# First loads of a decoder block issued from two queues, and the passes of its first two k-tiles in another order

## The chip, the core and the metric

The kernel runs on one core of one Trainium2 chip. The metric is the device time of one execution, in microseconds; lower is better. Five engines work side by side, each through its own list of instructions in order: TensorE (PE in the profile, with its weight loads as PEld), VectorE (DVE), ScalarE (ACT), GpSimd (POOL) and SyncE (SP). They wait for each other by semaphores. Data come from device memory by DMA, through 16 DMA engines; a DMA is issued as an instruction on one engine's list, its queue.

## The reference

A decoder block with 512 tokens and a model width of 1024: two token mixers side by side, retention and forgetting attention, merged by gates, and then a SwiGLU feed-forward. What the change touches is the first line of it, the normalised input times the combined input projection:

```
h = rmsnorm(x, g_mix[l])
z = h @ w_in[l]
q_r, k_r, v_r, gt_r, q_f, k_f, v_f, f_f, a_r, a_f = split_cols(z)
```

The first group of columns that the kernel computes is q_r and k_r together, 512 columns for all 512 tokens.

## The kernel before

Matrix products run in a split form. Each float32 operand is taken apart into a high part, rounded to the format `float32r`, and a low part, the remainder; `three` (line 164) issues three matmuls, or passes, for one product: high x high, high x low and low x high. For the input that means `xh` and `xl`, for the weights `wh` and `wl` (`h` and `l` in the code).

The head of the kernel is lines 174 to 212. The input comes transposed, in NK = 8 k-tiles of 128 rows (`xT[:, k, :]`, 256 KB each). For each k-tile the loop at line 182 issues a load of x into `xf`, a load of 512 columns of weights into `raw` (for the last four k-tiles the buffer is called `spare`), and for the first k-tile a small load `ce`, 16 KB of constants that holds the scale `g_mix`. Then it makes four parts: ScalarE makes `xh` (line 189), VectorE makes `wh` (a cast, line 190), `xl` (line 191) and `wl` (line 194). All these loads are issued by SyncE, x and weights in turn.

Before them ScalarE does a copy of one element, `cold` (line 106), ahead of which a load of the activation table stands; TensorE runs eight warm-up matmuls on zeros (line 125).

The loop at line 196 then runs the products: for each of eight k-tiles and four token tiles t the three passes, 96 matmuls of 512 columns, into four accumulators (two banks called `sc`, two called `tp`). The program is laid out by a scheduler that sets the order of each engine's instructions by when it thinks that their inputs are there; only where `pinned[0]` is set does `in_order` (line 65) keep the matmuls in the order in which they are written. In the head it is not set.

After the head come the loads of the next group's weights (`ahead`, line 202), the input in row form for the sums of squares (`xs`, lines 203 to 207), and tables. The next group (`tok_group`, line 227) accumulates into banks called `acc`; its weights are split by ScalarE (line 151) and VectorE (line 152). Everything after that is the same in both kernels.

The buffers are reused by rotation: three pairs `wh` and `wl`, two `raw`, so that a cast for the next group waits until TensorE has read an older one. DMAs take eight semaphores in turn, so an issue can wait until an earlier load with the same semaphore has landed.

Of the kernel before, what the change touches and what calls it, by code (L numbers as in the profile page):

```python
# [17 lines left out]
P = 128  # L18
D = 1024
S = 512  # L20
NT = S // P
NK = D // P
# [31 lines left out]
def block_kernel(ctx: ExitStack, tc, x, xT, c_early, c_tab, c_late, w_qf, w_tok, w_a, w_y, w_o, w_gu, w_dn, out):  # L54
    nc = tc.nc
# [3 lines left out]
    pinned = [False, None]  # L59

    def after(ins, prev):

        tc.add_manual_dep(ins.ins, prev.ins.name, mybir.DependencyInfo(mybir.DependencyClass.NoSync, mybir.DependencyReason.DATA), reason="order")

    def in_order(ins):
        if pinned[0]:
            if pinned[1] is not None:
                after(ins, pinned[1])
            pinned[1] = ins

    def mm(o, **kw):
        in_order(nc.tensor.matmul(o, **kw))  # L72
# [4 lines left out]
    def f32(ap):  # L77
        return ap.bitcast(F32)
# [12 lines left out]
    def bank(tag):  # L91
        return ps.tile([P, 512], F32, name=tag, tag=tag, bufs={"acc": 4, "sc": 2, "tp": 2}[tag])

    ce = cst.tile([P, C_EARLY], F32, name="ce")
# [8 lines left out]
    nc.vector.memset(warm, 0.0)  # L103
    cold = sm.tile([P, 2], F32, name="cold", tag="cold", bufs=1)
    nc.gpsimd.memset(cold, 0.0)
    nc.scalar.copy(out=cold[:, 0:1], in_=cold[:, 1:2])
    ctab = cst.tile([P, C_TAB], F32, name="ctab")
    ident, tri, mask = (ctab[:, o:o + P] for o in (T_ID, T_TRI, T_MASK))

# [31 lines left out]
    def load_w(src, width=1024):  # L141
        pool, bufs = next_pool(raw_pools, 0)
        raw = pool.tile([P, WU if pool is wp else 1024], F32, name="raw", tag="raw", bufs=bufs)
        nc.sync.dma_start(out=raw[:, :width], in_=src)
        return raw
# [9 lines left out]
    def split_w(src, width=1024):  # L155
        return split_raw(load_w(src, width), width)

    def gmix(k):
        return ce[:, C_GMIX + k:C_GMIX + k + 1]
# [4 lines left out]
    def three(o, sh, sl, mh, ml, first, last):  # L164
        mm(o, lhsT=sh, rhs=mh, start=first, stop=False)
        mm(o, lhsT=sh, rhs=ml, start=False, stop=False)
        mm(o, lhsT=sl, rhs=mh, start=False, stop=last)
# [6 lines left out]
    xh = hp.tile([P, NK, S], F32R, name="xh")  # L174
    xl = hp.tile([P, NK, S], F32R, name="xl")
# [6 lines left out]
    for k in range(NK):  # L182
        u, cs = k // 2, slice(k % 2 * 512, k % 2 * 512 + 512)
        raw, xk, (h, l) = raws[u][:, cs], xf[k // 4][:, k % 4, :], first_units[u]
        nc.sync.dma_start(out=xk, in_=xT[:, k, :])
        if k == 0:
            nc.sync.dma_start(out=ce, in_=c_early)
        nc.sync.dma_start(out=raw, in_=w_tok[2, u, :, cs])
        act(out=xh[:, k, :], in_=xk, func=AF.Copy, scale=gmix(k))
        first = nc.vector.tensor_copy(out=h[:, cs], in_=raw)  # L190
        low = stt(out=xl[:, k, :], in0=xk, scalar=gmix(k), in1=f32(xh)[:, k, :], op0=ALU.mult, op1=ALU.subtract)
        if k == 0:
            after(low, first)
        tt(out=l[:, cs], in0=raw, in1=f32(h)[:, cs], op=ALU.subtract)
    accs = [bank(("sc", "tp")[t // 2]) for t in range(NT)]
    for k in range(NK):
        h, l = first_units[k // 2]
        cs = slice(k % 2 * 512, k % 2 * 512 + 512)
        for t in range(NT):
            tq = slice(t * P, (t + 1) * P)  # L200
            three(accs[t], xh[:, k, tq], xl[:, k, tq], h[:, cs], l[:, cs], k == 0, k == NK - 1)
    ahead = [load_w(w_tok[3, u]) for u in range(2)]
    for t2 in range(2):
        nc.sync.dma_start(out=xs[t2], in_=x[t2 * 256:(t2 + 1) * 256].rearrange("(t p) d -> p t d", p=P))
# [367 lines left out]
    cs = ftok.tile([P, NT, FH], F32, name="cs")  # L572
# [131 lines left out]
    accs = [bank(("tp", "sc", "acc", "acc")[b // 2]) for b in range(8)]  # L704
# [8 lines left out]
    for k in range(NF):  # L713
        h, l = split_w(w_dn[k])
# [109 lines left out]
```

## Time and profile before

| | us |
|---|---|
| median of 3 runs | 738.85 |
| lowest and highest run | 738.72, 739.54 |
| the profiled execution | 739.33 |
| its span, first to last instruction | 737.2 |

The profiled execution is one run with the hardware profiler; 2.1 us of its time lie outside the span. Times in a row are microseconds from the start of the span. The timeline gives start, duration, engine, line, operation and names (written to <- read from), and in brackets the idle time before it and what ended that. The profile pipelines matmuls: one takes longer than the distance to the next one's start, and the distance is what the engine can sustain. The chain of waits is followed back from the last instruction, at each step to what released it.

### The profile page before, as it was taken

The numbers are of one execution on the slowest core, as the hardware profiler recorded it, in microseconds if no ns is written. First come the engines' busy times: TensorE is split into PE (matmuls) and PEld (weight loads), VectorE is DVE, ScalarE is ACT, GpSimd is POOL, SyncE is SP. The second block draws the span as 40 slices with busy tenths as digits, with TensorE's granted clock in tenths as the row PEclk, the third lists the DMA queues.
The fourth block names the chain that finished last, engine by engine and source line by source line (L and its number), as shares of the span: only waits on it lengthen the run. The fifth ranks groups of instructions, "written<-read, shape, count | busy, mean of one in ns | idle before, by whom it ended". The sixth has DMA issues, their size and how long they took to land.

```text
span 737.2 us, 8828 instructions
## 1 busy us (share of the span) xinstructions
PE 729.2 (99%) x3430; PEld 596.5 (81%) x3430; DVE 367.6 (50%) x630; ACT 260.1 (35%) x389; POOL 108.8 (15%) x112
## 2 busy tenths in 40 slices
PE   8999999999999999999999999999999999999998
PEld 5888998778777788888888888888888887888886
DVE  6434567656878653454676343333333336323213
ACT  4532433347766732333433222222222233232210
POOL 0253502222211000000311110111110111000000
PEclk9999999999999999999999999999999999999999
DMA  8542222233321133336244223233232332332203
GB/s 315 202 123 78 88 76 62 68 121 105 104 73 55 36 107 93 108 86 222 92 143 135 94 86 114 86 100 101 87 110 90 94 107 85 97 104 85 86 0 115
DMA packets 23353, 76.20 MB, mean 103 GB/s; under 512 B 2696, under 2 KB 3080, under 8 KB 23312
## 3 DMA queue, kind: packets, MB, share of 16 engines
q1 hardware_dynamic: 23312, 75.64, 32.4%
q8 instruction: 27, 0.44, 0.2%
q14 instruction: 14, 0.11, 0.0%
HBM read 73.52 MB, written 2.11 MB: 103 GB/s over the span
## 4 chain that ended last, share of the span: by engine, by line
PE 92%; DVE 4%; ACT 2%; issue 1%; DMA 1%; SPq 0%; DVEq 0%; ACTq 0%
PE acc L72 76%; PE sc L72 9%; PE tp L72 6%; PE tp L75 2%; DVE wl L152 1%; ACT pr L482 1%; DMA xf<-in_xT_dram 1%; DVE pr L480 0%; ACT wh L151 0%; ACT pT L499 0%; DVE pr L484 0%; DVE tq L459 0%; ACT tq L458 0%; DVE og L382 0%; DVE up L688 0%
## 5 line engine op out<-in xcount | busy, mean ns | idle before, releaser
L151 ACT CAST wh<-raw 128x1024 fp32r<-128x1024 f32 (+1 forms) x118 | 123.8, 1052 | 381.4 <-PE acc L72 315.2
L152 DVE TENSOR_TENSOR wl<-raw,wh 128x1024 fp32r<-128x1024 f32 (+1 forms) x118 | 154.0, 1306 | 195.1 <-ACT wh L151 193.7
L72 PE MATMUL acc<-xgh,wh 128*128 128x512 f32 x352 | 137.4, 390 | 0.0
L72 PE MATMUL acc<-xgh,wl 128*128 128x512 f32 x352 | 136.9, 389 | 0.0
L72 PE MATMUL acc<-xgl,wh 128*128 128x512 f32 x352 | 136.9, 389 | 0.0
L72 PEld LDWEIGHTS acc<-xgh,wh 128*128 128x128 f32 x352 | 66.1, 188 | 13.9 <-issue 0.2
L72 PEld LDWEIGHTS acc<-xgh,wl 128*128 128x128 f32 x352 | 66.1, 188 | 13.8
L72 PEld LDWEIGHTS acc<-xgl,wh 128*128 128x128 f32 x352 | 66.1, 188 | 13.8 <-issue 0.2
L72 PE MATMUL acc<-wh,xh 128*128 128x512 f32 (+2 forms) x192 | 70.0, 364 | 0.0
L72 PE MATMUL acc<-wh,xl 128*128 128x512 f32 (+2 forms) x192 | 68.2, 355 | 0.0
L72 PE MATMUL acc<-wl,xh 128*128 128x512 f32 (+2 forms) x192 | 68.0, 354 | 0.0
L689 POOL TENSOR_TENSOR pf<-up,gt 128x512 f32<-128x512 f32 x22 | 38.2, 1756 | 199.3 <-DVE up L688 199.3
L72 PE MATMUL acc<-xh,wh 128*128 128x512 f32 x128 | 51.7, 404 | 0.0
L72 PE MATMUL acc<-xh,wl 128*128 128x512 f32 x128 | 50.0, 391 | 0.0
L72 PE MATMUL acc<-xl,wh 128*128 128x512 f32 x128 | 49.9, 390 | 0.0
L72 PEld LDWEIGHTS acc<-wh,xh 128*128 128x128 f32 x192 | 36.2, 188 | 5.5 <-issue 0.3
L72 PEld LDWEIGHTS acc<-wh,xl 128*128 128x128 f32 x192 | 36.2, 189 | 5.2
L72 PEld LDWEIGHTS acc<-wl,xh 128*128 128x128 f32 x192 | 36.2, 189 | 4.6
L72 PE MATMUL acc<-ph,wl 128*128 128x512 f32 x88 | 34.2, 389 | 0.0
L72 PE MATMUL acc<-pl,wh 128*128 128x512 f32 x88 | 34.2, 389 | 0.0
L72 PE MATMUL acc<-ph,wh 128*128 128x512 f32 x88 | 33.9, 389 | 0.0
L666 POOL TENSOR_TENSOR sqs<-sqs,sq 128x512 f32<-128x512 f32 x7 | 11.6, 1650 | 124.5 <-ACT sq L665 124.2
(215 smaller groups left out, 1121.8 us busy)
## 6 DMA issues: line engine op xcount, KB each, us to landing
raw<-in_w_gu_dram SPq DMA_DIRECT2D x44, 512.0 KB, 3.6
raw<-in_w_dn_dram SPq DMA_DIRECT2D x22, 512.0 KB, 3.6
raw<-in_w_tok_dram SPq DMA_DIRECT2D x16, 512.0 KB, 3.7
raw<-in_w_a_dram SPq DMA_DIRECT2D x16, 512.0 KB, 3.6
raw<-in_w_y_dram SPq DMA_DIRECT2D x8, 512.0 KB, 3.5
raw<-in_w_o_dram SPq DMA_DIRECT2D x8, 512.0 KB, 3.8
xf<-in_xT_dram SPq DMA_DIRECT2D x8, 256.0 KB, 5.4
xs<-in_x_dram SPq DMA_DIRECT2D x2, 1024.0 KB, 8.4
```

Of the source, the lines that this page charges most:

```text
L72: in_order(nc.tensor.matmul(o, **kw))
L75: in_order(nc.tensor.transpose(out=o, in_=src, identity=ident))
L151: nc.scalar.copy(out=h[:, :width], in_=raw[:, :width])
L152: tt(out=l[:, :width], in0=raw[:, :width], in1=f32(h)[:, :width], op=ALU.subtract)
L482: fox["last"] = act(out=pr[:, :n], in_=pr[:, :n], func=AF.Exp, scale=-1.0, bias=nm, accum_out=rs)
L666: gp.tensor_tensor(out=sqs, in0=sqs, in1=sq2, op=ALU.add)
L689: gp.tensor_tensor(out=pf[:, 2 * f2 + m2, :], in0=up, in1=gts[m2], op=ALU.mult)
```

## The change

The small load `ce` and the weights of the first four k-tiles are issued by ScalarE; x and the later weights stay on SyncE. The one-element copy on ScalarE stands behind its first two issues. The products of the first two k-tiles are written pass by pass over the four token tiles, in the order high x high, low x high, high x low (of x and weights), and the matmuls of the head are pinned to the written order.

```diff
--- before.py
+++ after.py
@@ -103,7 +103,6 @@
     nc.vector.memset(warm, 0.0)
     cold = sm.tile([P, 2], F32, name="cold", tag="cold", bufs=1)
     nc.gpsimd.memset(cold, 0.0)
-    nc.scalar.copy(out=cold[:, 0:1], in_=cold[:, 1:2])
     ctab = cst.tile([P, C_TAB], F32, name="ctab")
     ident, tri, mask = (ctab[:, o:o + P] for o in (T_ID, T_TRI, T_MASK))
 
@@ -184,8 +183,10 @@
         raw, xk, (h, l) = raws[u][:, cs], xf[k // 4][:, k % 4, :], first_units[u]
         nc.sync.dma_start(out=xk, in_=xT[:, k, :])
         if k == 0:
-            nc.sync.dma_start(out=ce, in_=c_early)
-        nc.sync.dma_start(out=raw, in_=w_tok[2, u, :, cs])
+            nc.scalar.dma_start(out=ce, in_=c_early)
+        (nc.scalar if k < 4 else nc.sync).dma_start(out=raw, in_=w_tok[2, u, :, cs])
+        if k == 0:
+            nc.scalar.copy(out=cold[:, 0:1], in_=cold[:, 1:2])
         act(out=xh[:, k, :], in_=xk, func=AF.Copy, scale=gmix(k))
         first = nc.vector.tensor_copy(out=h[:, cs], in_=raw)
         low = stt(out=xl[:, k, :], in0=xk, scalar=gmix(k), in1=f32(xh)[:, k, :], op0=ALU.mult, op1=ALU.subtract)
@@ -193,12 +194,19 @@
             after(low, first)
         tt(out=l[:, cs], in0=raw, in1=f32(h)[:, cs], op=ALU.subtract)
     accs = [bank(("sc", "tp")[t // 2]) for t in range(NT)]
+    pinned[0] = True
     for k in range(NK):
         h, l = first_units[k // 2]
         cs = slice(k % 2 * 512, k % 2 * 512 + 512)
-        for t in range(NT):
-            tq = slice(t * P, (t + 1) * P)
-            three(accs[t], xh[:, k, tq], xl[:, k, tq], h[:, cs], l[:, cs], k == 0, k == NK - 1)
+        tqs = [slice(t * P, (t + 1) * P) for t in range(NT)]
+        if k < 2:
+            for n, (a, b) in enumerate(((xh, h), (xl, h), (xh, l))):
+                for t in range(NT):
+                    mm(accs[t], lhsT=a[:, k, tqs[t]], rhs=b[:, cs], start=k + n == 0, stop=False)
+        else:
+            for t in range(NT):
+                three(accs[t], xh[:, k, tqs[t]], xl[:, k, tqs[t]], h[:, cs], l[:, cs], False, k == NK - 1)
+    pinned[0] = False
     ahead = [load_w(w_tok[3, u]) for u in range(2)]
     for t2 in range(2):
         nc.sync.dma_start(out=xs[t2], in_=x[t2 * 256:(t2 + 1) * 256].rearrange("(t p) d -> p t d", p=P))
```

ScalarE from its first instruction on (`junk` is the sum of squares, the CAST the split of the next group's weights). Before:

```order
L106 ACT_TABLE_LOAD
L106 COPY cold<-cold 128x1
L189 ACTIVATE xh<-xf,ce 128x512 x8
L151 CAST wh<-raw 128x1024 x2
L207 ACTIVATE junk,ss_85<-xs 128x1024 x4
```

The changed kernel:

```order
L186 DMA ce<-in_c_early_dram 128x32
L187 DMA raw<-in_w_tok_dram 128x512
L189 ACT_TABLE_LOAD
L189 COPY cold<-cold 128x1
L190 ACTIVATE xh<-xf,ce 128x512
L187 DMA raw<-in_w_tok_dram 128x512
L190 ACTIVATE xh<-xf,ce 128x512
L187 DMA raw<-in_w_tok_dram 128x512
L190 ACTIVATE xh<-xf,ce 128x512
L187 DMA raw<-in_w_tok_dram 128x512
L190 ACTIVATE xh<-xf,ce 128x512 x5
L150 CAST wh<-raw 128x1024
```

The weights of k-tiles 1 to 3 are each issued behind one `xh`; the table load stands behind two issues. Behind the last of these rows two sums of squares now come before the second CAST, and two after it.

VectorE from its first cast on: each k-tile has a CAST (`wh`), an `xl` and a `wl`. Before:

```order
L190 CAST wh<-raw 128x512
L191 SCALAR_TENSOR_TENSOR xl<-xf,ce,xh 128x512
L194 TENSOR_TENSOR wl<-raw,wh 128x512
L191 SCALAR_TENSOR_TENSOR xl<-xf,ce,xh 128x512
L190 CAST wh<-raw 128x512
L194 TENSOR_TENSOR wl<-raw,wh 128x512
L190 CAST wh<-raw 128x512
L191 SCALAR_TENSOR_TENSOR xl<-xf,ce,xh 128x512
L194 TENSOR_TENSOR wl<-raw,wh 128x512
```

The changed kernel:

```order
L191 CAST wh<-raw 128x512
L195 TENSOR_TENSOR wl<-raw,wh 128x512
L192 SCALAR_TENSOR_TENSOR xl<-xf,ce,xh 128x512 x2
L191 CAST wh<-raw 128x512
L192 SCALAR_TENSOR_TENSOR xl<-xf,ce,xh 128x512
L195 TENSOR_TENSOR wl<-raw,wh 128x512
L191 CAST wh<-raw 128x512
L192 SCALAR_TENSOR_TENSOR xl<-xf,ce,xh 128x512
L195 TENSOR_TENSOR wl<-raw,wh 128x512
```

For k-tile 0 `wl` now stands ahead of `xl`; for k-tile 1 `xl` stands ahead of the cast, and the `xl` of k-tile 2 ahead of the `wl` of k-tile 1. On SyncE five loads of x now come first, then weights and x in turn. On TensorE, after four high x high passes of k-tile 0, the other passes come in fours, for k-tile 1 too; from k-tile 2 on its order is what it was.

## Rows read from the trace of the kernel before

**Rows 1.** The page, parts 1 and 4: busy time by engine, the chain's shares by engine.

```profile
PE 729.2 (99%) x3430; PEld 596.5 (81%) x3430; DVE 367.6 (50%) x630; ACT 260.1 (35%) x389; POOL 108.8 (15%) x112
...
PE 92%; DVE 4%; ACT 2%; issue 1%; DMA 1%; SPq 0%; DVEq 0%; ACTq 0%
```

**Rows 2.** Windows: us, busy per engine (x instructions), granted clock, DMA share, GB/s.

```profile
9.76:28.68 18.92, 18.92 (x83) 15.69 (x84) 11.91 (x20) 9.78 (x14) 0.00 (x0) 1.00 0.98 385
```

**Rows 3.** The chain that ended last, in time: start us, us, what.

```profile
2.10 5.00 DMA xf<-in_xT_dram
```

**Rows 4.** Timeline of SyncE's queue: start us, us, engine, line, operation, names.

```profile
0.73 0.38 SPq L185 DMA_DIRECT2D xf<-in_xT_dram  x1
...
1.17 0.42 SPq L187 DMA_DIRECT2D ce<-in_c_early_dram  x1
...
1.64 0.42 SPq L188 DMA_DIRECT2D raw<-in_w_tok_dram  x1
...
2.58 0.43 SPq L188 DMA_DIRECT2D raw<-in_w_tok_dram  x1
```

**Rows 5.** DMA issues at 0.73, 1.17, 1.64, 2.10, 2.58: count, KB, us to landing.

```profile
xf<-in_xT_dram SPq DMA_DIRECT2D x1, 256.0 KB, 3.0
ce<-in_c_early_dram SPq DMA_DIRECT2D x1, 16.0 KB, 2.7
raw<-in_w_tok_dram SPq DMA_DIRECT2D x1, 256.0 KB, 3.2
xf<-in_xT_dram SPq DMA_DIRECT2D x1, 256.0 KB, 5.0
raw<-in_w_tok_dram SPq DMA_DIRECT2D x1, 256.0 KB, 5.2
```

**Rows 6.** Timeline of ScalarE.

```profile
0.73 1.28 ACT L106 ACT_TABLE_LOAD   x1 [0.73 <-PEq L813]
...
3.95 0.72 ACT L189 ACTIVATE xh<-xf,ce 128x512 fp32r<-128x512 f32 x1 [1.74 <-DMA ce<-in_c_early_dram]
...
7.13 0.72 ACT L189 ACTIVATE xh<-xf,ce 128x512 fp32r<-128x512 f32 x1 [2.46 <-DMA xf<-in_xT_dram]
...
23.44 1.05 ACT L151 CAST wh<-raw 128x1024 fp32r<-128x1024 f32 x1 [4.38 <-PE tp L72]
...
24.39 1.05 ACT L207 ACTIVATE junk<-xs 128x1024 bf16<-128x1024 f32 x1
```

**Rows 7.** Timeline of VectorE, first two k-tiles.

```profile
4.82 0.43 DVE L190 CAST wh<-raw 128x512 fp32r<-128x512 f32 x1 [3.69 <-DMA raw<-in_w_tok_dram]
...
5.16 0.74 DVE L191 SCALAR_TENSOR_TENSOR xl<-xf,ce,xh 128x512 fp32r<-128x512 f32 x1
...
5.83 0.68 DVE L194 TENSOR_TENSOR wl<-raw,wh 128x512 fp32r<-128x512 f32 x1
...
8.56 0.42 DVE L190 CAST wh<-raw 128x512 fp32r<-128x512 f32 x1
```

**Rows 8.** Timeline of TensorE, warm-up to the next group.

```profile
1.18 3.60 PE L72 MATMUL tp<-warm 128*128 128x512 bf16 x8 [1.18 <-DVE warm L103]
...
5.39 0.70 PE L72 MATMUL sc<-wh,xh 128*128 128x512 f32 x2 [0.61 <-DVE wh L190]
...
6.56 0.50 PE L72 MATMUL sc<-wl,xh 128*128 128x512 f32 x1
...
9.12 0.47 PE L72 MATMUL sc<-wh,xh 128*128 128x512 f32 x1 [0.46 <-ACT xh L189]
...
9.76 0.50 PE L72 MATMUL sc<-wl,xh 128*128 128x512 f32 x1 [0.16 <-DVE wl L194]
...
28.68 0.39 PE L72 MATMUL acc<-wh,xh 128*128 128x512 f32 x1
```

**Rows 9.** Windows of one microsecond, same columns as Rows 2.

```profile
5.00:6.00 1.00, 0.61 (x3) 0.55 (x4) 1.00 (x3) 0.00 (x0) 0.00 (x0) 1.00 0.54 160
...
9.00:10.00 1.00, 0.71 (x2) 0.43 (x3) 0.99 (x3) 0.38 (x2) 0.00 (x0) 1.00 1.06 397
```

## The prediction, made before the changed kernel ran

> **What bounds the kernel now.** I read first the page: TensorE is busy 99% of the span and 92% of the chain that ended last is its own [rows 1]. So the change can gain only where TensorE still waits, and it touches only the head, where the first group of projections is fed. The timeline of TensorE gives the size of that [rows 8]. Eight warm-up matmuls run from 1.18 to 4.78. The first real matmul starts at 5.39, the 96 matmuls of the group follow, and the next group starts at 28.68. From 9.76 on nothing stalls: 83 matmuls in 18.92 us, 0.228 us each [rows 2]. The 96 need 96 x 0.228 = 21.9 us; they got 28.68 - 5.39 = 23.3. So 1.4 us are stalls behind 5.39, and 0.6 us lie idle between 4.78 and 5.39: **2.0 us is all there is**, 0.27% of the time.
>
> Who ended those waits: the first matmul waited for the cast of the first weights [rows 8], which VectorE began at 4.82, as soon as they had landed [rows 7]. The second pass began at 6.56, when `wl` was made: 4 x 0.228 = 0.9 after 5.39 would have been 6.30. The eight matmuls from 6.56 end by 8.4, but k-tile 1 starts at 9.12, and its second matmul waits until 9.76 for the low part. The chain shows why: the second block of x, issued at 2.10, took 5.00 us [rows 3], `xh` of k-tile 1 starts only at 7.13 [rows 6], and VectorE's cast for k-tile 1 stands behind the `xl` that needs it, at 8.56 [rows 7]. With a stall-free run from k-tile 1 on, the end of the head stands as if k-tile 1 had started at 9.76 - 0.23 = **9.53**. The whole sum is the difference from that.
>
> **The change, part by part.** *Loads on two queues.* SyncE issues one load per 0.47 us (0.73, 1.17, 1.64) [rows 4]. Now `ce` and the first weights go out on ScalarE, at 0.73 and about 1.20 by the same spacing, and SyncE's first five rows are all blocks of x: the second goes from 2.10 to 1.17, 0.9 us earlier. Issue to landing was 3.0 to 3.2 us for the first loads, 5.0 and 5.2 for the next two [rows 5]. In one microsecond of that stretch the DMA engines moved only 160 GB/s, against 397 later [rows 9]; what caused that I can't see. First weights: not before 1.20 + 3.0 = 4.2, not after that plus the 256 KB of x beside them, which at 397 GB/s is 0.65: 4.85, what it was. I take 4.4, the 3.2 of the same load before. The first real matmul came 0.57 after the cast began [rows 7, 8], so it starts near 4.95, 0.4 earlier. If the first few then run at the warm-up's spacing of 3.60/8 = 0.45, that costs up to 0.9 us in the first pass; half of it is hidden by the wait that follows.
>
> *Table load behind the issues.* 1.28 us from 0.73 [rows 6], now from about 1.65, so ready by 3.1 with its copy. `xh` starts no earlier than its data, 0.73 + 3.0 = 3.73, so this is free with 0.6 to spare. `ce`, which ended the wait at 3.95, no longer decides.
>
> *Passes of k-tile 0.* TensorE now runs four high x high, four with `xl`, four with `wl`. But the order on VectorE is cast, `wl`, `xl`: the part needed second is made third. Either way both parts are wanted after four matmuls, so nothing is gained here: `wl` was started 1.01 after the cast and took 0.68, 1.69 in all [rows 7]; now `xl` is the last, 1.7 after 4.4, so the second pass starts at 6.1 and k-tile 0 ends at 6.1 + 8 x 0.228 = **7.9**. With the bounds of the landing: 7.7 to 8.4.
>
> *Weights of k-tile 1 behind `xh`.* This is the step that decides. The second weights were issued at 2.58 [rows 4]; now the issue stands on ScalarE behind the first `xh`. That one started at 3.95 and took 0.72 [rows 6], so the issue is at 3.95 if ScalarE's queue goes on while `xh` computes, 4.67 if not. No row shows a load issued on ScalarE. The Trainium skill (Perfetto Trace Analysis, section DVE / Act Engine Instruction) has the sequencer free for the next instruction once one is pushed into the wait queue; that would be 3.95; no row before shows it. Behind `xh`, too, stand the third and fourth weights, which k-tiles 2 and 3 need 2.7 and 5.5 us after k-tile 1: covered. From issue to landing the bounds are 3.2 (an idle queue, as the first weights) and 5.2 (as these very weights, with a backlog before them) [rows 5]. Its own queue is empty, though the engines still carry blocks of x, so I go a third of the way: 3.9, landing at 7.85. TensorE follows 0.57 later: **8.4**. Bounds: 3.95 + 3.2 + 0.57 = 7.7 and 4.67 + 5.2 + 0.57 = 10.4.
>
> *Passes of k-tile 1.* High x high and the `xl` pass cover 8 x 0.228 = 1.8 us. The low part of the weights is made after the cast and one `xl`, 1.69 behind the cast's start, and TensorE starts 0.57 behind it: cover 2.4 against 1.69. The stall between 9.12 and 9.76 is gone, and its return needs `xh` of k-tile 2 to be late by 0.7. K-tile 2 starts 12 x 0.228 = 2.7 after k-tile 1; VectorE makes three operations per tile, 1.7 us, and keeps ahead.
>
> *Behind the head.* On ScalarE the second cast for the next group, at 23.44 [rows 6], now stands behind two squares, 2 x 1.2 us. TensorE needs it 24 matmuls into that group, 28.68 + 5.5 = 34.2: covered by 7 us even if the head ends 2 us sooner. All else keeps its order; the gain passes to the end because TensorE has no further wait on anything of the head.
>
> **Sum.** K-tile 1 starts at max(7.9, 8.4) = 8.4 instead of 9.53: **1.1 us less**. The profiled execution took 739.33 (span 737.2 and 2.1 around it); with 1.1 less it would be 738.2. It lies 0.5 above the median of the runs shown, and against that median the forecast is 738.85 - 1.1 = 737.7. What a measurement of this kernel can tell from no change is about 0.2%, 1.5 us: the forecast is a gain below that.
>
> **Rivals.** *The early feed holds fully.* The second weights land by 7.3 and k-tile 0 is the bound: k-tile 1 starts at 7.7 to 7.9, a gain of 1.6 to 1.8 and at the very most the 2.0 of the whole, time 736.85 to 737.25. For it: the x blocks leave earlier and the new queue is empty. Against it: 3.2 us was seen only before the slow microsecond of [rows 9]. Chance 0.26.
>
> *Both queues issue one at a time.* The 0.47 us spacing is then shared: the first weights stand third or fourth, at 1.64 to 2.1, so the first matmul comes at 5.4 to 5.9 and k-tile 0 ends at 8.4 to 8.8; the second weights leave at about 4.4, land at 8.3 and k-tile 1 starts at 8.9. Gain 0.6; landing in 4.5 us instead of 3.9 leaves none: 738.25 to 738.85. For it: the 0.42 us of every issue row is spent somewhere [rows 4]. Against it: no row shows two queues at once. The Trainium skill names this mechanism (Perfetto Trace Analysis, section DMA Instruction — HWDGE (DVE, Sync)): the descriptor generator is shared and locked for exclusive use. By that rule two queues gain nothing in issue rate. A second sentence of the skill (DMA: Bandwidth & Descriptors, section Issuing engines are not separate DMA queues) says that issuing from several engines saves only the sequencer's time, usually small. Chance 0.22.
>
> *Slower: the second weights are late.* Their issue waits for `xh` to end (4.67), and the five blocks of x that SyncE sends off first, 1.25 MB or 3.3 us at 397 GB/s, go ahead of them. They land at 4.67 + 5.2 = 9.9, with another 0.65 to 2 us for the backlog at 10.5 to 11.9, and TensorE starts k-tile 1 at 11.1 to 12.5: 1.6 to 2.9 us slower, 740.4 to 741.8. It decides from a landing at 8.96: later than that is a loss. Against it: the engines would have to serve one queue before the other. Chance 0.05, and 0.03 for a milder form between 0 and 1.5 us slower.
>
> **How the numbers follow.** Forecast (gain 0.5 to 1.6) 0.44, full feed 0.26, one at a time 0.22, late weights 0.08. Faster by over 0.2% is most of the full feed and the best edge of the forecast: 0.23 + 0.05 = 0.28. Slower by over 0.2% is the late weights at their price: 0.05. Within: 0.67. The range reaches from the full feed's 736.85, rounded to 736.8, to a small loss of 0.25 us, 739.1; beyond it lie the late weights and the two ends, under 0.2.
>
> **What would show it.** Right: no wait on the first weights after 5.0, the `raw` issue on ScalarE at about 4.0, the cast of k-tile 1 near 7.9, the next group at 27.6 instead of 28.68, and no gap inside k-tile 1. One at a time: issue rows of near 0.9 us where both queues issue. Wrong: k-tile 1 past 9.53, or a new wait of TensorE behind 30 us.

## The result: slower, by a later and slower start

The changed kernel took 741.58 us (median of 8 runs, 740.22 to 742.2) beside 739.25 for the kernel before (8 runs, 738.72 to 740.72) on the same chip. The ratio is 1.0025, with a 95% interval of 1.0014 to 1.0036: slower by about 1.9 us, where 737.7 was forecast. (The ratio goes by the means of the runs; the medians are 2.3 us apart.) Every later run was timed beside the kernel before on its own chip, where that kernel's median lay between 739.3 and 739.9, so it is the ratios that can be set side by side. The profiled execution took 741.52 (span 739.6), against 739.33 (span 737.2) before.

All of it is lost in the head. The next group of projections starts at 31.32 instead of 28.68 [rows 8], 2.64 later; from there to the end the changed kernel needs 710.20 us (741.52 - 31.32), the kernel before 710.65, 0.45 less. The timeline of TensorE after (start, duration, engine, line, operation, names, idle time before and its releaser):

```profile
...
6.84 1.19 PE L72 MATMUL sc<-wh,xh 128*128 128x512 f32 x2 [2.06 <-DVE wh L191]
7.83 1.05 PE L72 MATMUL tp<-wh,xh 128*128 128x512 f32 x2
...
12.10 0.76 PE L72 MATMUL sc<-wh,xh 128*128 128x512 f32 x2
...
31.32 0.39 PE L72 MATMUL acc<-wh,xh 128*128 128x512 f32 x1
```

Three things differ from [rows 8]. The first real matmul comes at 6.84 instead of 5.39, after 2.06 us of idleness. The matmuls that follow stand as far apart as the warm-ups: k-tile 0 takes 12.10 - 6.84 = 5.26 us, 0.56 from the first matmul to the second and 0.427 for each of the next eleven, where 0.228 is the rate of [rows 2]; 512 columns in 0.427 us are 1.2 GHz, the lower of the two levels. And from 12.10 on nothing stalls, as the last of these stretches shows (busy time and count of TensorE first, then the other engines, granted clock, DMA share, GB/s):

```profile
4.78:6.84 2.06, 0.00 (x0) 0.03 (x1) 0.54 (x2) 0.77 (x2) 0.00 (x0) 1.00 1.01 383
6.84:12.10 5.26, 5.26 (x13) 4.10 (x14) 4.04 (x8) 2.74 (x4) 0.00 (x0) 1.00 1.04 386
12.10:31.32 19.22, 19.22 (x85) 15.91 (x84) 12.65 (x28) 7.95 (x12) 0.00 (x0) 1.00 0.83 313
```

So k-tile 1 starts at 12.10 and not at the effective 9.53: 2.57 of the 2.64. The clock column prints 1.00 in the middle stretch, as it does over the warm-ups; there the distance of the matmuls tells the level, not the column.

Who was waited for stands on ScalarE's and VectorE's timelines after, to be held against [rows 5 to 7]:

```profile
0.74 0.40 ACTq L186 DMA_DIRECT2D ce<-in_c_early_dram  x1
1.17 0.45 ACTq L187 DMA_DIRECT2D raw<-in_w_tok_dram  x1
1.65 1.28 ACT L189 ACT_TABLE_LOAD   x1 [1.65 <-PEq L821]
...
4.11 0.72 ACT L190 ACTIVATE xh<-xf,ce 128x512 fp32r<-128x512 f32 x1 [0.97 <-DMA ce<-in_c_early_dram]
4.11 0.35 ACTq L187 DMA_DIRECT2D raw<-in_w_tok_dram  x1
```

```profile
6.27 0.43 DVE L191 CAST wh<-raw 128x512 fp32r<-128x512 f32 x1 [5.14 <-DMA raw<-in_w_tok_dram]
...
9.60 0.43 DVE L191 CAST wh<-raw 128x512 fp32r<-128x512 f32 x1 [0.85 <-DMA raw<-in_w_tok_dram]
```

The first weights were issued half a microsecond earlier than before and landed 1.45 later. The DMA issues after, of the first 1.6 us and of 4 to 5 us (count, KB each, median us from issue to landing):

```profile
xf<-in_xT_dram SPq DMA_DIRECT2D x2, 256.0 KB, 3.8
raw<-in_w_tok_dram ACTq DMA_DIRECT2D x1, 256.0 KB, 5.1
ce<-in_c_early_dram ACTq DMA_DIRECT2D x1, 16.0 KB, 3.3
...
raw<-in_w_tok_dram ACTq DMA_DIRECT2D x1, 256.0 KB, 5.5
```

My theory behind the result: (a) the weights on the second queue share the DMA engines with five blocks of x that SyncE now sends off at once, four of which nobody needs yet; (b) the longer idleness after the warm-ups leaves TensorE at 1.2 GHz for the first pass. Rivals: ScalarE's queue is slow in itself; the new order of the passes costs; the second weights are late only because their issue stands behind `xh`.

### The profile page after: what moved, and what is told of

Read it like the earlier page. It is cut to its first block, busy times and chain, and to the rows that moved or that the text cites. A ratio compares the mean times of both kernels' runs of the same rounds, so it can differ in the third digit from the quotient of the medians.

```text
span 739.6 us, 8826 instructions
## 1 busy us (share of the span) xinstructions
PE 731.0 (99%) x3430; PEld 598.5 (81%) x3430; DVE 366.8 (50%) x630; ACT 259.9 (35%) x389; POOL 109.1 (15%) x112
## 4 chain that ended last, share of the span: by engine, by line
PE 96%; DVE 2%; DMA 1%; ACT 1%; issue 0%; ACTq 0%; DVEq 0%
PE acc L72 78%; PE sc L72 10%; PE tp L72 6%; PE tp L75 2%; DMA raw<-in_w_tok_dram 1%; ACT wh L150 0%; DVE wl L151 0%; DVE og L390 0%; DVE up L696 0%; DVE pl L726 0%; DVE n4a L120 0%; DVE n4a L119 0%; DVE n4y L121 0%; ACT pr L490 0%; DVE og L396 0%
```

## The experiments

### Which half of the change costs

`e1_loads_only` has the loads of the changed kernel and the loop of matmuls of the kernel before, not pinned. `e2_passes_only` has the loads of before and the new loop.

> The two queues of the changed kernel with the matmul order of the kernel before (no pinning, three passes per token tile). Theory: the first weights land late because ScalarE's queue shares the DMA engines with the blocks of x, TensorE idles about 2 us after its warm-up (4.8 to 6.8), and then runs its first matmuls at half rate, 0.427 us apart, as in the warm-up, until about 12.3. So this kernel is slow too: next group at 31.0 to 31.6, time 2 to 2.7 us over the kernel before. Rival: the new order of the passes makes the matmuls slow; then the matmuls here are 0.228 apart, the next group starts at 28.7 to 29.2, and the time is that of before within 0.5.

> The loads of the kernel before (all on SyncE) with the new pinned order of the passes. Theory: first real matmul near 5.4 as before, all matmuls 0.228 apart, the wait inside k-tile 1 (9.12 to 9.76) gone, next group at 28.0 to 28.4, time 0.3 to 0.7 below the kernel before, too little to be told from no change. Rival (the order of the passes is slow): matmuls of the first two k-tiles 0.427 apart, next group after 30.5, 2 us slower.

The loads alone: 740.39 us, ratio 1.0015 [1.0006, 1.0025], 1.1 us slower where I had expected 2 to 2.7. The first weights land 4.9 us behind their issue, the first matmul starts at 6.64 and the first eight matmuls run at the low clock, where the changed kernel had twelve; the next group starts at 30.23 and not past 31.0, as I had expected.

```profile
6.06 0.43 DVE L191 CAST wh<-raw 128x512 fp32r<-128x512 f32 x1 [4.94 <-DMA raw<-in_w_tok_dram]
6.64 1.19 PE L72 MATMUL sc<-wh,xh 128*128 128x512 f32 x2 [1.86 <-ACT xh L190]
```

The passes alone: 739.25 us, 0.9993 [0.9984, 1.0002], no difference that can be told. The passes are not the loss. But I had expected full rate from the first matmul and a next group by 28.4, and in the profiled execution the first eight matmuls were 0.43 apart, with the feed of the kernel before and only 0.72 us of idleness:

```profile
5.50 1.19 PE L72 MATMUL sc<-wh,xh 128*128 128x512 f32 x2 [0.72 <-DVE wh L190]
6.49 1.05 PE L72 MATMUL tp<-wh,xh 128*128 128x512 f32 x2
7.34 1.05 PE L72 MATMUL sc<-wh,xl 128*128 128x512 f32 x2
...
9.05 0.68 PE L72 MATMUL sc<-wl,xh 128*128 128x512 f32 x2
```

The next group came at 29.10. So the level of the clock behind the warm-ups is not settled by the idle time alone.

### How much is the clock

```diff
-WARM = 8
+WARM = 16   # in the changed kernel: e3_after_warm16
+WARM = 3    # in the kernel before: e4_before_warm3
```

> The changed kernel with 16 warm-up matmuls instead of 8, so that TensorE is busy until shortly before the first weights are there. Theory (the clock): the first real matmul still starts near 6.8, but runs at full rate; the next group starts at 28.7 to 29.0 instead of 31.32, and the time is 2.3 to 2.7 us under the changed kernel, that of before within 0.4. If the warm-ups run beyond 6.8 it is later by as much. Rival (something else than the idle time makes the first passes slow): still 0.427 apart until 12.3, no gain over the changed kernel.

> The kernel before with 3 warm-up matmuls instead of 8: only the idle time of TensorE ahead of the first real matmul grows, from 0.6 to about 2.9 us, loads and passes are untouched. Theory: the first real matmul starts at 5.4 and runs at 0.427 us spacing for several us; next group at 30.5 to 31.4, time 1.8 to 2.7 us over the kernel before. Rival (the loads or the passes are the cause, not the idle time): 28.7 and no change.

With 16 warm-ups the changed kernel takes 740.13 us, 1.0007 [0.9998, 1.0017]: from 1.9 us of loss some 0.5 is left, and that can no longer be told from none. TensorE runs at full rate from its first real matmul on, and what remains is the late data:

```profile
1.18 4.94 PE L72 MATMUL tp<-warm 128*128 128x512 bf16 x16 [1.18 <-DVE warm L103]
6.49 0.70 PE L72 MATMUL sc<-wh,xh 128*128 128x512 f32 x2 [0.37 <-ACT xh L190]
...
7.79 0.73 PE L72 MATMUL sc<-wh,xl 128*128 128x512 f32 x2
...
9.96 0.70 PE L72 MATMUL sc<-wh,xh 128*128 128x512 f32 x2
...
13.49 0.50 PE L72 MATMUL sc<-wl,xh 128*128 128x512 f32 x1 [0.30 <-DVE wl L195]
```

K-tile 1 starts at 9.96, still behind 9.53, and k-tile 2 waits for `wl` until 13.49; the next group starts at 29.72 and not by 29.0, as I had expected. Late data cost 29.72 - 28.68 = 1.04 here, so about 1.6 of the 2.64 went with the clock. Holding the clock alone does not make the change a gain.

In the other direction the kernel before with three warm-ups, 2.9 us idle and its own loads, runs twelve matmuls at 0.43 and starts the next group at 29.91, 1.23 later: 740.2 us, 1.0007 [0.9997, 1.0016].

```profile
5.55 1.19 PE L72 MATMUL sc<-wh,xh 128*128 128x512 f32 x2 [2.90 <-DVE wh L190]
...
29.91 0.39 PE L72 MATMUL acc<-wh,xh 128*128 128x512 f32 x1
```

The price of the low clock appears in the head without any of the change, though less of it than the 1.8 to 2.7 us that I had expected, and in the time it is too small to be told from none. Both runs change the amount of warm-up work together with the idle time, so they show what the clock costs and not which of the two sets it.

Then both kernels once more, unchanged:

> The kernel before, unchanged, profiled a second time. If the level of TensorE's clock behind the warm-up is settled by the program, the next group starts at 28.7 again and the first matmuls are 0.228 us apart, as in the first profile. If it differs from one execution to the next, the first eight to twelve matmuls may now be 0.427 apart and the next group starts up to 1.5 us later, near 30.

> The changed kernel, unchanged, profiled a second time. If the landing of the first weights, 5.1 us behind their issue, is settled by the two queues, it is 5.0 to 5.2 again and the cast of the first weights starts near 6.2. If it was an accident of one execution, it is nearer 3.5. The next group starts at 31.3 if the first matmuls are again at the low clock, near 29 if not.

The kernel before took 738.65 in this profile, at full rate from the first matmul at 5.51; its second weights were cast at 7.79 instead of 8.56, and the next group started at 27.93, 0.75 earlier than in [rows 8]. The changed kernel took 740.42. Its first weights landed 4.7 us behind their issue, its first four matmuls ran at full rate, and then the clock fell; here the column shows it (window of 7.70 to 10.20):

```profile
6.42 0.70 PE L72 MATMUL sc<-wh,xh 128*128 128x512 f32 x2 [1.84 <-ACT xh L190]
6.96 0.63 PE L72 MATMUL tp<-wh,xh 128*128 128x512 f32 x2
7.72 1.22 PE L72 MATMUL sc<-wh,xl 128*128 128x512 f32 x2
```

```profile
7.70:10.20 2.50, 2.48 (x6) 2.02 (x7) 1.60 (x3) 1.10 (x3) 0.00 (x0) 0.50 1.01 354
```

Eight matmuls at half clock (from 7.72 to 11.20, the last of them partly) instead of twelve: k-tile 1 at 11.20, the next group at 30.29. The late landing is in both profiles of the changed kernel (5.1 and 4.7 us); the level of the clock, and so the size of the loss, differs between the two.

### Why the first weights land late

`e9_small_x` keeps every queue and its order, and cuts the bytes beside the weights: of the x blocks 1 to 7 it loads an eighth and leaves out the rest, which GpSimd fills with zeros.

```diff
-        nc.sync.dma_start(out=xk, in_=xT[:, k, :])
+        if k == 0:
+            nc.sync.dma_start(out=xk, in_=xT[:, k, :])
+        else:
+            nc.sync.dma_start(out=xk[:, 0:64], in_=xT[:, k, 0:64])
+            nc.gpsimd.memset(xk[:, 64:512], 0.0)
```

> The changed kernel, but of the x blocks 1 to 7 only an eighth is loaded (the rest is filled with zeros, so the output is not the reference's). Same queues, same order, same number of loads; in the first microseconds SyncE's queue carries 0.38 MB instead of 1.25. If the first weights come late because they share the DMA engines with those blocks, they land 3.0 to 3.6 us behind their issue, the cast starts at 4.2 to 4.8 and the first matmul at 4.8 to 5.4; the weights of k-tile 1 land 3 to 4 us behind theirs. If ScalarE's queue is slow by itself, or the small rows of the constants ahead of the weights hold it up, the first weights again land about 5.1 us behind their issue and the cast starts near 6.2.

The first weights landed 3.6 us behind their issue, at the edge of what sharing gave (3.0 to 3.6) and far from 5.1. Their cast started at 4.83 and the first matmul at 5.41, as in the kernel before (4.82 and 5.39), at full rate:

```profile
xf<-in_xT_dram SPq DMA_DIRECT2D x1, 256.0 KB, 3.3
raw<-in_w_tok_dram ACTq DMA_DIRECT2D x1, 256.0 KB, 3.6
xf<-in_xT_dram SPq DMA_DIRECT2D x1, 32.0 KB, 3.2
ce<-in_c_early_dram ACTq DMA_DIRECT2D x1, 16.0 KB, 3.5
...
raw<-in_w_tok_dram ACTq DMA_DIRECT2D x2, 256.0 KB, 5.3
```

ScalarE's queue is not slow in itself; the x blocks beside it are what held the weights. The bytes of each queue say it directly: from 1.6 to 4.7 us SyncE's queue moved 0.51 MB and ScalarE's 0.18 in the changed kernel, 0.43 and 0.28 here, and 0.28 MB is `ce` and the first weights whole. The second weights are another matter. They were issued at 4.24 and cast at 8.44, 4.2 us later, a little past the 3 to 4 that I had expected, and the third took still longer. By then SyncE's queue carries `spare`, the weights of later k-tiles (issued at 3.05, 4.82 and 5.81), which may be why; no run takes that apart. The next group started at 29.06, and the single execution took 739.12.

`e6_raw_first_w10` puts the first weights ahead of `ce` on ScalarE, with ten warm-ups:

```diff
+        (nc.scalar if k < 4 else nc.sync).dma_start(out=raw, in_=w_tok[2, u, :, cs])
         if k == 0:
             nc.scalar.dma_start(out=ce, in_=c_early)
-        (nc.scalar if k < 4 else nc.sync).dma_start(out=raw, in_=w_tok[2, u, :, cs])
```

> The changed kernel with the first weights issued ahead of the constants on ScalarE's queue, and 10 warm-up matmuls. If it is the small rows of the constants, each waiting a turn behind a 2 KB row of x, that hold up the first weights, they land at 4.2 to 4.6 here and the cast starts then, 1.5 us earlier than in the changed kernel (the first xh then waits for the constants until 5 or later). If it is the blocks of x on SyncE's queue alone, the first weights land at 5.3 or later and the gain is under 1 us. By either theory this kernel is not faster than the one before by more than 0.5 us, since the second and third weights still share with the x blocks (cast of k-tile 1 at 8.5 to 9.5).

740.76 us, 1.0014 [1.0005, 1.0022]. The weights still took 4.9 us, and now the 16 KB of `ce` took 5.4 and held every `xh`:

```profile
raw<-in_w_tok_dram ACTq DMA_DIRECT2D x1, 256.0 KB, 4.9
ce<-in_c_early_dram ACTq DMA_DIRECT2D x1, 16.0 KB, 5.4
```

```profile
6.64 0.72 ACT L190 ACTIVATE xh<-xf,ce 128x512 fp32r<-128x512 f32 x1 [3.51 <-DMA ce<-in_c_early_dram]
```

The first matmul came at 7.42. In this kernel the second weights also went out early, at 1.71, so three loads stood on ScalarE's queue ahead of the first `xh`. A small load behind a large one was as late as the large one, and the order on ScalarE's queue was not the cause.

`e11_second_early` asks whether the second weights are late because they are issued behind `xh`:

```diff
-        (nc.scalar if k < 4 else nc.sync).dma_start(out=raw, in_=w_tok[2, u, :, cs])
+        if k != 1:
+            (nc.scalar if k < 4 else nc.sync).dma_start(out=raw, in_=w_tok[2, u, :, cs])
         if k == 0:
+            nc.scalar.dma_start(out=raws[0][:, 512:1024], in_=w_tok[2, 0, :, 512:1024])
```

The cast for k-tile 1 is also kept behind the first `xl`, where it stands in the changed kernel.

> The changed kernel, but the weights of k-tile 1 are issued on ScalarE's queue right behind the first ones, near 1.65 instead of 4.1 to 4.4 behind the first xh. If they are late in the changed kernel because of that late issue, they now land by 7 and the cast for k-tile 1 follows the first xl directly, near 7.7, at least 1.4 earlier than the 9.2 and 9.6 of the two profiles of the changed kernel; no gap of TensorE is left ahead of k-tile 1. If the five x blocks ahead of them in the DMA engines set the landing, whenever they are issued, the cast again starts past 9. The first weights may land later by the 0.65 us that 256 KB more take at 397 GB/s, near 6.5. The time: 740 to 741 by the first theory, since the low clock of the first pass is still there; 741 to 742 by the second.

741.16 us, 1.0022 [1.0012, 1.0032]. Issued at 1.65, the second weights took 6.6 us and landed at about 8.2, where I had expected 7 by the first theory; VectorE came to them at 8.79, without a wait. So both theories hold a part: an issue 2.5 to 2.8 us earlier brought the landing forward by only 1.0 to 1.4 (from 9.23 and 9.60), and the rest went into a longer way to landing. TensorE had no gap ahead of k-tile 1, but that proves little: k-tile 0 ran at half rate until 12.88, and the changed kernel had no gap there either. And the first weights paid for it, by 0.8 to 1.2 us against the two profiles of the changed kernel, where I had expected 0.65:

```profile
7.05 0.43 DVE L193 CAST wh<-raw 128x512 fp32r<-128x512 f32 x1 [5.93 <-DMA raw<-in_w_tok_dram]
...
8.12 0.75 DVE L194 SCALAR_TENSOR_TENSOR xl<-xf,ce,xh 128x512 fp32r<-128x512 f32 x1
8.79 0.42 DVE L193 CAST wh<-raw 128x512 fp32r<-128x512 f32 x1
```

The first weights took 5.9 us, and the x of k-tile 1 came at 6.84 (5.69 in the changed kernel). What was sent off early took its share from what was needed first. The stretches of DMA traffic from 0.70 to 4.70 and 4.70 to 6.70 say the same (last column GB/s): before, after, and this kernel, two rows each:

```profile
0.70:4.70 4.00, 3.52 (x8) 1.04 (x8) 0.27 (x1) 2.20 (x3) 0.45 (x3) 1.00 0.62 185
4.70:6.70 2.00, 1.38 (x6) 0.81 (x6) 1.69 (x3) 0.00 (x0) 0.00 (x0) 1.00 0.69 215
```

```profile
0.70:4.70 4.00, 3.52 (x8) 1.04 (x8) 0.27 (x1) 2.07 (x3) 0.45 (x3) 1.00 0.69 173
4.70:6.70 2.00, 0.08 (x1) 0.00 (x0) 0.43 (x1) 0.85 (x2) 0.00 (x0) 1.00 1.00 374
```

```profile
0.70:4.70 4.00, 3.52 (x8) 1.03 (x8) 0.27 (x1) 2.16 (x3) 0.45 (x3) 1.00 0.65 166
4.70:6.70 2.00, 0.08 (x1) 0.00 (x0) 0.00 (x0) 0.04 (x1) 0.00 (x0) 1.00 1.00 361
```

Up to 4.70 the kernel before moves 4.0 x 185 = 0.74 MB, the changed one 0.69 and this one 0.66. In these two, more queues and earlier issues moved no byte sooner. They only mixed the bytes, so that the engines run at 374 GB/s in the next two microseconds while TensorE stands idle.

### What does gain

If mixing is the loss, only `ce` should leave SyncE's queue: 16 KB that take an issue of 0.47 us ahead of the first weights. Four kernels take that apart, with ten warm-ups (`w10`) or eight:

```diff
-        (nc.scalar if k < 4 else nc.sync).dma_start(out=raw, in_=w_tok[2, u, :, cs])
+        nc.sync.dma_start(out=raw, in_=w_tok[2, u, :, cs])
```

This edit of the changed kernel makes `e10_ce_only_w8`, and `e5_ce_only_w10` with `WARM = 10`; `e7_passes_w10` and `e8_before_w10` are `e2_passes_only` and the kernel before with `WARM = 10`.

> Only the 16 KB of constants go to ScalarE's queue; x and all weights go out on SyncE in turn, so the first weights are second on SyncE's queue; new order of the passes; 10 warm-up matmuls. Theory (weights on a second queue are late because they share the DMA engines with everything SyncE has sent off): here the first weights land 3.0 to 3.4 us after an issue at 1.2, the cast starts at 4.2 to 4.6 instead of 5.9 to 6.3, the next group starts at 27.6 to 28.5, and the time is 0.7 to 1.5 us below the kernel before. Rival (any load on the second queue disturbs the first ones, or weights landing is limited by the total bytes): cast at 4.8 or later, no gain over the kernel before.

> Loads of the kernel before, new order of the passes, 10 warm-up matmuls. Theory: the two more warm-up matmuls close most of the idle time before the first real one, so the full rate is there at the first pass or within 1 us of it in more executions: next group at 28.0 to 28.6, median 0.6 to 1.3 us below the kernel before and less spread between runs. Rival (the spread has another cause): spread and median as with 8 warm-ups and the new passes alone, 739.25.

> The kernel before with 10 warm-up matmuls, nothing else. Theory: as above without the passes: next group at 28.6 to 29.0, median 0.2 to 0.8 us below the kernel before, 0.3 to 0.6 above the one with the new passes. Rival (warm-ups don't matter between 8 and 10): no change.

> Only the constants on ScalarE's queue, x and all weights in turn on SyncE's, the changed order of the passes, and eight warm-ups as in the two kernels. If the loads and the order make the gain that was seen with ten warm-ups (737.8), the time is 737.5 to 738.3 here too. If the two more warm-ups made it, by holding TensorE's clock, the first matmuls are 0.427 apart, the next group starts 1.5 to 2 us later than with ten, and the time is 739.3 to 740.

| | us | ratio to before, 95% | next group |
|---|---|---|---|
| `e5_ce_only_w10` | 737.83 | 0.9974 [0.9964, 0.9984] | 27.37 |
| `e10_ce_only_w8` | 737.69 | 0.9980 [0.9969, 0.9991] | 27.39 |
| `e7_passes_w10` | 738.92 | 0.9990 [0.9981, 0.9999] | 29.02 |
| `e8_before_w10` | 739.27 | 0.9994 [0.9986, 1.0003] | 28.23 |

`ce` alone on ScalarE, with the new passes, beats both kernels: it gains some 1.5 to 1.9 us on the one before. More warm-ups alone are worth nothing that can be told, and the gain is there without them. The new passes with ten warm-ups gain 0.7 us, an interval that only just leaves out none. The loads of this kernel with the old passes were not run, so how the gain divides between the two is not shown. With eight, though, three of eleven executions took 739.5 to 739.9 and the other eight 737.2 to 737.8; with ten, all nine lie between 737.3 and 738.2. I take the three for executions with the low clock, but none of them was profiled. In the profile of `e10_ce_only_w8` SyncE issues x and weights in turn, from the second on one place earlier than before:

```profile
1.17 0.42 SPq L187 DMA_DIRECT2D raw<-in_w_tok_dram  x1
...
2.10 0.43 SPq L187 DMA_DIRECT2D raw<-in_w_tok_dram  x1
...
4.78 0.43 DVE L191 CAST wh<-raw 128x512 fp32r<-128x512 f32 x1 [3.66 <-DMA raw<-in_w_tok_dram]
...
7.16 0.42 DVE L191 CAST wh<-raw 128x512 fp32r<-128x512 f32 x1
```

```profile
5.35:27.39 22.04, 22.04 (x97) 18.02 (x98) 14.95 (x25) 11.29 (x16) 0.00 (x0) 1.00 1.01 382
```

The first weights land no earlier than before (cast at 4.78 against 4.82; 4.93 in `e5_ce_only_w10`, where I had expected 4.2 to 4.6), so the gain does not come from where I had put it. But the second are cast at 7.16 instead of 8.56, and the 96 matmuls run in 22.04 us, nearly without a stall, where they got 23.3 before. Here only the 16 KB of `ce` mix in, and the bytes do come sooner: 0.80 MB up to 4.70, beside the 0.74 of the kernel before. In `e7_passes_w10`, with all loads on SyncE, `xh` of k-tile 1 starts only at 7.86, VectorE's cast behind its `xl` at 9.29, and TensorE begins k-tile 1 at 9.86 after a wait of 0.95 us: the new order of the passes has nothing to work on earlier, and the next group starts at 29.02 and not at 28.0 to 28.6, as I had expected.

## Why the prediction was wrong, step by step

| step of the prediction | forecast | after, two profiles |
|---|---|---|
| first weights issued | 1.20 | 1.17, 1.17 |
| their cast | 4.4 (at most 4.85) | 6.27, 5.85 |
| first matmul behind that cast | 0.57 | 0.57, 0.57 |
| second weights issued | 3.95 (at most 4.67) | 4.11, 4.44 |
| their cast | 7.85 (bounds 7.15 to 9.87) | 9.60, 9.23 |
| k-tile 1 starts | 8.4 | 12.10, 11.20 |
| stall inside k-tile 1 | gone | gone, gone |
| next group | 27.6 | 31.32, 30.29 |

**What held.** Both queues issued side by side, at 0.37 to 0.45 us each, so the rival of queues that issue one at a time fell: SyncE sent five blocks of x in 2.3 us while ScalarE issued its two. The shared and locked generator that the prediction cites for that rival left no mark in these rows. ScalarE's list goes on while `xh` computes: the issue of the second weights stands at 4.11 and 4.44, the very start of `xh` (4.11 and 4.43), and not at its end. The sequencer's rule cited in the prediction would even allow an issue while `xh` still waits for its data; in both profiles it came only when that wait was over. The table load was free, but `ce` was not out of the way, as the prediction had it: in both profiles it landed last and ended the wait of the first `xh`, so the issue came 0.16 and 0.49 after the forecast 3.95. The passes took away the stall in k-tile 1. TensorE had no new wait behind the head; the rest even came 0.45 shorter. That difference is in every profile with `ce` on ScalarE (710.06 to 710.29 us behind the start of the next group) and in none with it on SyncE (710.58 to 710.72). Half or more of it is a single wait of TensorE, some 180 us into that stretch, of 0.23 to 0.29 us for a copy on ScalarE, which is in all six profiles with `ce` on SyncE and in none of the nine others. In the kernel before:

```profile
208.86 0.66 PE L75 MATMUL tp<-ctab,pr 128*128 128x128 f32 x4 [0.29 <-ACT pT L499]
```

The rest lies outside the span (2.1 us before, 1.8 to 2.05 with `ce` on ScalarE). What moves either is open. So some 0.45 of the gain of the two kernels with only `ce` on ScalarE does not come from the head.

**The first weights: the step that failed first.** I took the 3.2 us of the same load before and bounded it by 256 KB of x beside it, 4.85 at most. The bound was wrong: ScalarE's load ran beside five blocks, not one. The landing of 5.1 (4.7 in the second profile) is what sharing gives, as loading an eighth of x showed (3.6). For the second weights the same backlog stood among the bounds; for the first it did not, though the part on the loads says in its own words that SyncE's first five rows are now all x. The Trainium skill (DMA: Bandwidth & Descriptors, section Issuing engines are not separate DMA queues), cited in the prediction for the issue rate, says in the same place that loads from different engines run on the same DMA engines and interleave. The traces agree with both halves: nothing but issue time was saved (0.74 MB before and 0.69 MB after by 4.70), and the interleaving was the cost (by then 0.18 MB for ScalarE's queue beside 0.51 for SyncE's). I had weighed only the first half.

**The second weights: the size.** 5.5 and 4.8 us from issue to landing, where I went "a third of the way" between 3.2 and 5.2 to 3.9. The empty queue on which that rested counts for nothing, since the DMA engines behind it were full (383 GB/s between 4.78 and 6.84).

**The clock: the term left out.** The prediction has one sentence on it, up to 0.9 us in the first pass, half hidden, on the ground that four matmuls might run at the warm-ups' distance. Twelve did, and eight in the second profile. With the second weights cast at 9.60, k-tile 1 could have started at 9.60 + 0.57 = 10.17, 0.64 behind 9.53; the other 1.93 of the 2.57 lie in the low clock (at full rate some 0.6 of it would come back as the stall in k-tile 2 that the run with 16 warm-ups shows). In the second profile the same sum gives 9.23 + 0.57 = 9.80, 0.27 behind 9.53, and 1.40 for the clock. The likeliest trigger is the idleness before the first matmul, which went from 0.61 to 2.06 with the late weights. In the six profiles with the longest idleness there (both of the changed kernel and those of `e1`, `e4`, `e6` and `e11`; 1.84 to 2.90 us) eight to thirteen matmuls ran at half rate. In the nine others (0.93 us at most) it was eight matmuls in `e2_passes_only`, the first one or two in `e7_passes_w10`, and none in the rest. What makes `e2_passes_only` the exception stays open, and so does the trigger: no run changes the idle time and leaves loads and warm-ups as they were.

**The slower rival.** Its range, 740.4 to 741.8, holds the result, but its mechanism does not: it has the second weights landing past 10.5 and TensorE at full rate. Its sign did come: a landing behind 8.96 in both profiles (9.60 and 9.23). That alone is worth the 0.64 and 0.27 above; it was the clock that brought the time into the range, which is luck. I gave it 0.05 because the engines "would have to serve one queue before the other". They need not; it is enough that they serve both in turn. The range of the whole ended at 739.1 for that reason.

## What to carry to other kernels

In this head a second issuing queue saved issue time and reordered the bytes. Where the DMA engines are full before the first data are in, a load moved earlier makes another later, so count the bytes in flight ahead of the first needed load, on all queues, before counting issues. Move only small loads off the busy queue and keep the large ones in turn in the order in which they are needed. And cost a later first matmul twice: by its own delay, and by the matmuls that may then run at half rate.

## What the runs showed of the hardware that was not expected

The granted clock behind the same eight warm-ups is not the same in each profiled execution: the kernel before showed full rate in both its profiles, the passes alone 0.43 for eight matmuls with the same feed, the changed kernel once half rate from the first matmul on and once full rate for four matmuls and then half. Landings vary too: the second block of x, with the loads of the kernel before, let its `xh` start at 7.13 and 6.36 in the two profiles of that kernel, and between 5.96 and 7.86 in all six with these loads; the cast of the second weights stands behind it (8.56 and 7.79), and the whole execution followed, 739.33 and 738.65. One profiled execution of this kernel therefore tells its head to no better than about 0.7 us, as much as most of the effects that the prediction added up, and the gain of the last kernels rests on their runs and not on one profile each. Two profiles of one kernel may come from two chips, and a part of this may be the chip; but the eight runs of the changed kernel in the result, on one chip, spread over 2.0 us as well, with mean granted clocks from 0.997 to 1.000. And 16 KB can take 5.4 us to land, when 256 KB stand before them on the same queue and more on another.
